# Two dense blocks on one core: second halves of weights later in the order, and a gated delta rule woven by another deal

## The chip, the cores and the metric

The kernel runs on one core of a Trainium2 chip. The metric is the device time of one execution in microseconds (us). Engines are named as in the profile: PE is TensorE's matmul, PEld its weight load, DVE is VectorE, ACT is ScalarE, POOL is GpSimd, SP is SyncE, whose queue issues the loads of the weights. Each engine takes its instructions in the order in which the program lists them.

## The reference, cut to what matters

Two blocks run one after the other on 256 tokens of width 1024. The first (attention and a mixture of 32 experts) is not touched. The second has two layers; the mixer of its first layer is a gated delta rule, of its second a block attention with rotary embedding ("moba"), and each is followed by a SwiGLU network.

```python
def gated_deltanet(x, w_in, w_conv, a_log, dt_bias, norm_g, w_out):
    proj = x @ w_in
    qkv, z, b_logit, a_in = jnp.split(proj, [...], axis=-1)
    qkv = jax.nn.silu(causal_depthwise_conv(qkv, w_conv))   # 4 taps, each channel by itself
    q, k, v = jnp.split(qkv, [GDN_QK, 2 * GDN_QK], axis=-1)
    q = l2_normalize(split_heads(q, nh)) * GDN_DK ** -0.5   # 8 heads of 128
    k = l2_normalize(split_heads(k, nh))
    v = split_heads(v, nh).astype(F32)
    beta = jax.nn.sigmoid(...)
    g = -(jnp.exp(a_log) * jax.nn.softplus(a_in + dt_bias))
    o = chunk_gated_delta_rule(q, k, v, g, beta)            # per head: triangular solve, recurrence
    o = o * lax.rsqrt(jnp.mean(o * o, -1, keepdims=True) + NORM_EPS) * norm_g
    o = o * jax.nn.silu(z)
    return o.reshape(bsz, seq, GDN_V) @ w_out

def second_block(x, ...):
    h = x
    for i in range(2):
        mix = gated_deltanet(h, ...) if i == 0 else moba_attention(h, ...)
        h = layer_norm(DEEPNORM_ALPHA * h + mix, ln1_g[i], ln1_b[i])
        h = layer_norm(DEEPNORM_ALPHA * h + swiglu(h, f_w13[i], f_w2[i]), ln2_g[i], ln2_b[i])
    return h
```

## The kernel before, in words

**Weights.** Every float32 product is made of three rounded products: a weight is split into a first half `wh` (ACT copies it to fp32r, line 1221: below "the cast") and a second half `wl` (the weight less `wh`, line 1224 on DVE, or on POOL while `hv.pool` is set: below "the second part"). `Stream` (lines 1204 to 1241) does this unit by unit: a unit is a quarter of a weight tile of up to 2 MB, and a ring of two places in SBUF holds the tiles. `_emit` lists the cast and the second part of one unit; after the last unit of a tile it calls `ring.free`, which issues the next load on SP's queue. `get` first fills a queue of units up to `ahead` + 1 and hands out the oldest.

**The delta rule** (`gdn`, from line 1444). The eight heads go in four pairs. `project(p)` makes q, k and v of a pair's two heads (48 steps of 768 columns on PE) and puts a generator `conv4` (line 1579) of each head on the list `late`: three first taps on ACT (line 1586), nine further taps on DVE (line 1584), then one SiLU on ACT (line 1595). `gates` also stands on `late`. `tick()` advances every generator on `late` by one step. `chunks(p)` (line 1609), below "the chain", is the delta rule of one pair: 26 steps, in each of which PE works on what DVE or ACT made in the step before. Its first two steps transpose (line 1620) and square (line 1623, ACT) the two heads, its third transposes the values (line 1629); the two buffers of the PSUM tile `tp` are used in turn, so the third step waits until ACT has finished the first head's squares and copy. POOL then takes the inverse root (line 328), lines 1657 and 1660 make the triangular matrices, lines 1677 to 1703 solve five levels (`X` and `W` in the trace: lines 1693 and 1703 on DVE), and lines 1718 to 1754 give the output.

**`weave`** (lines 1760 to 1788) sets the order by rounds. In a round each live chain advances by one step, and then a generator of other work ("the fill") is run for its share. The chains start in rounds 4, 12, 27 and 35. The fills are the projections of pairs 1, 2 and 3 (to be done by rounds 8, 23 and 31), the two other groups of z (round 45) and the first part of the output projection (round 65). The share is a fill's whole work over its rounds. After more than TICK = 1000 columns of fill comes a `tick`. Where a chain starts, `late` is emptied first. All of this stands in a manual schedule: on every engine the order of the program is the order of the queue.

**Boundaries** (`boundary`, lines 1300 to 1325) run the layer norm by an order written out by hand, also a manual schedule on PE, DVE and ACT: `... l01 b11 c00 h00 s10 f10 f11 x10 l10 x11 l11 h10`. The step `c00` takes four units from the stream for the next stage's first tile, `h00` multiplies them with the first 128 tokens, `s10`, `f10`, `f11` finish the norm of the other 128 tokens on DVE, `x10` and `x11` transpose them (line 413), `l10` and `l11` make their second halves (line 417), `h10` multiplies them. Outside manual schedules a planner orders the instructions.

Of the kernel before, what the change touches and what calls it, by code (L numbers as in the profile page):

```python
# [16 lines left out]
OP = mybir.AluOpType  # L17
# [20 lines left out]
TICK = 1000  # L38
# [4 lines left out]
LATE = 4  # L43
END = 7
SPLITS = 8
AHEAD = 4
FILL = 8


ORDER = "p00 p01 a00 b00 a01 b01 s00 p10 q11 f00 x00 r11 a10 f01 x01 l00 b10 a11 l01 b11 c00 h00 s10 f10 f11 x10 l10 x11 l11 h10"  # L50
# [150 lines left out]
def kernel(ctx: ExitStack, tc: tile.TileContext, a, out):  # L201
# [33 lines left out]
    for e in range(NE + 1):  # L235
        if e < NE:
            for k in range(4):
# [3 lines left out]
                src = w[:, k % 2 * TILE:(k % 2 + 1) * TILE].rearrange("p (k c) -> p k c", k=2)  # L241
# [29 lines left out]
    ring = Ring(nc, plan, both, n_block1, n_moe)  # L271
# [58 lines left out]
    def f32(ap):  # L330
        return ap.bitcast(F32)


    class Halves:


        def __init__(self, n_tiles, unit, first=0):

            self.first = first
            self.left, self.unit, self.ahead = n_tiles, unit, depth  # L340
            self.q, self.cur, self.pos = [], None, 0

        def _emit(self):
            if self.cur is None:
                if not self.left:
                    return False
                self.left -= 1
                self.cur, self.pos = ring.get(), 0
            src = self.cur[:, self.pos:self.pos + self.unit]
            shp = list(src.shape)  # L350
            n = int(np.prod(shp[1:]))
            wh = split.tile([128, 1024], F32R, name="wh")
            wl = split.tile([128, 1024], F32R, name="wl")
            if len(shp) == 4:
                s2 = src.rearrange("p a b c -> p (a b c)")
            else:
                s2 = src.rearrange("p a b -> p (a b)")
            nc.scalar.activation(wh[:, :n], s2, AF.Copy)  # L358
            eng = nc.gpsimd if self.first > 0 else nc.vector
            self.first -= 1  # L360
            eng.tensor_tensor(wl[:, :n], s2, f32(wh[:, :n]), op=OP.subtract)  # L361
            v = lambda t: t[:, :n].rearrange("p (u c) -> p u c", u=self.unit)
            self.q.append((v(wh), v(wl)))
            self.pos += self.unit
            if self.pos >= self.cur.shape[1]:
                self.cur = None
                ring.free()
            return True

        def get(self):  # L370
            while len(self.q) <= self.ahead and self._emit():
                pass
            return self.q.pop(0)
# [320 lines left out]
    def begun(g):  # L694

        next(g)
        go = lambda: next(g, None)
        return {H1: go, H2: go}


    rest = begun(qk_b(psB, 0, qB, 8))
# [5 lines left out]
    rest = begun(qk_b(ps, 1, kB, 2))  # L707
    rest = {0: restq, H1: rest[H1], H2: rest[H2]}
# [3 lines left out]
    for hp in range(4):  # L712
# [3 lines left out]
        for g in range(3):  # L716
            ps = mm_tiles()
            dense_tok(ps, hT_h, hT_l, hv, 8, 384, 2, hooks=rest)
            rest = {}
            if g < 2:  # L720
                rest = begun(qk_a(ps, g, (QA, KA)[g][hp]))
# [482 lines left out]
    class Stream:  # L1204


        def __init__(self):
            self.q, self.cur, self.pos, self.ahead = [], None, 0, AHEAD
            self.n, self.pool = 0, 0

        def _emit(self):
            if self.cur is None:
                if ring.at not in ring.tiles:
                    return False
                self.pos, self.cur = 0, ring.get()
                self.unit = {256: 4, 1024: 1}.get(self.cur.shape[2], 2)
            src = self.cur[:, self.pos:self.pos + self.unit].rearrange("p a b -> p (a b)")
            n = src.shape[1]
            w = splitp.tile([128, 2, 1024], F32R, name="wh")
            wh, wl = w[:, 0, :n], w[:, 1, :n]  # L1220
            nc.scalar.activation(wh, src, AF.Copy)  # L1221
            self.n = self.n + 1
            eng = nc.gpsimd if self.n % 3 < self.pool else nc.vector
            eng.tensor_tensor(wl, src, f32(wh), op=OP.subtract)  # L1224
            self.pos += self.unit
            if self.pos >= self.cur.shape[1]:
                ring.free()
                self.cur = None
            v = lambda t: t.rearrange("p (u c) -> p u c", u=self.unit)
            self.q.append((v(wh), v(wl)))  # L1230
            return True

        def fill(self, n):

            while len(self.q) < n and self._emit():
                pass

        def get(self):
            self.fill(self.ahead + 1)
            return self.q.pop(0)  # L1240

    hv = Stream()
# [45 lines left out]
    def mm3(o, xh, xl, wh, wl, k, t, nk):  # L1288

        ts_ = slice(t * 128, (t + 1) * 128)  # L1290
        nc.tensor.matmul(o, xh[:, k, ts_], wh, start=k == 0, stop=False)  # L1291
        nc.tensor.matmul(o, xh[:, k, ts_], wl, start=False, stop=False)  # L1292
        nc.tensor.matmul(o, xl[:, k, ts_], wh, start=False, stop=k == nk - 1)  # L1293
# [50 lines left out]
    class OutProj:  # L1344
# [29 lines left out]
        def second(self, ln, pool, head, row=None):  # L1374
            hv.fill(FILL - 4)
            boundary(Residual(ln, pool, row=row), lambda t, n: self.part(t, n, 0 if t else 2, 4), self.ps, head)
# [22 lines left out]
    def ffn(i, ln, last, head):  # L1399
        with tc.tile_pool(name="ff1_%d" % i, bufs=1, reuse_waits="tile") as fr, tc.tile_pool(name="ff2_%d" % i, bufs=2, reuse_waits="tile") as fw:  # L1400
# [24 lines left out]
            for k in range(22 - TAIL):  # L1425
                hv.ahead = min(FILL - 1, max(AHEAD, FILL - (22 - TAIL - k)))
                wh, wl = hv.get()
                for t in range(2):
                    for n in range(2):
                        c = slice(n * 512, (n + 1) * 512)  # L1430
                        mm3(pss[n][t], aT_h, aT_l, wh[:, 0, c], wl[:, 0, c], k, t, 22)
            hv.fill(FILL)
            hv.ahead = 0
# [10 lines left out]
    def gdn(head):  # L1444
        with tc.tile_pool(name="gd1", bufs=1, reuse_waits="tile") as gr, tc.tile_pool(name="gd2", bufs=2, reuse_waits="tile") as gw:
# [28 lines left out]
            zs, qkvs, op, oT, gated = [], {}, [], [], []  # L1474

            late = []

            def tick():
                late[:] = [g for g in late if next(g, 0) is None]
# [280 lines left out]
            def weave(chains, fills):  # L1760


                r, live, todo, base, done = 0, [], 0.0, 0, 0
                while chains or live or fills:
                    while chains and chains[0][0] <= r:
                        while late:
                            tick()
                        live.append(chunks(chains.pop(0)[1]))
                    if live:

                        hv.pool = 0

                    live = [g for g in live if next(g, 0) is None]
                    todo += fills[0][1] / (fills[0][0] - base) if fills else 0
                    while fills and todo > 0:
                        n = next(fills[0][2], None)
                        if n is None:
                            base = fills.pop(0)[0]
                            todo = 0 if base > r else todo
                            break  # L1780
                        todo -= n
                        done = done + n
                        if done > TICK:
                            done = 0
                            tick()
                    r += 1
# [266 lines left out]
```

## Time and profile before

| | us |
|---|---|
| median of 3 runs | 1931.11 |
| lowest, highest | 1929.81, 1931.31 |
| the profiled execution's own time | 1930.78 |
| its span, first to last instruction | 1929.1 |
| first block, to about | 1222 of the span |
| delta rule with its rounds, about | 1222 to 1422 |
| boundary, network, boundary | 1422 to 1630 |
| moba and boundary | 1630 to 1741 |
| network and end | 1741 to 1929 |

The rows further down come from the profile's page and from answers of the trace. A row of a timeline begins with its start and its duration; in brackets stands how long the engine was idle before it and which instruction released it. PEclk is the granted TensorE clock as a share of full speed.

### The profile page before, as it was taken

The numbers are of one execution on the slowest core, as the hardware profiler recorded it, in microseconds if no ns is written. First come the engines' busy times: TensorE is split into PE (matmuls) and PEld (weight loads), VectorE is DVE, ScalarE is ACT, GpSimd is POOL, SyncE is SP. The second block draws the span as 40 slices with busy tenths as digits, with TensorE's granted clock in tenths as the row PEclk, the third lists the DMA queues.
The fourth block names the chain that finished last, engine by engine and source line by source line (L and its number), as shares of the span: only waits on it lengthen the run. The fifth ranks groups of instructions, "written<-read, shape, count | busy, mean of one in ns | idle before, by whom it ended". The sixth has DMA issues, their size and how long they took to land.

```text
span 1929.1 us, 26325 instructions
## 1 busy us (share of the span) xinstructions
PE 1856.5 (96%) x11094; PEld 1243.2 (64%) x11094; DVE 856.2 (44%) x1633; ACT 597.6 (31%) x1060; POOL 98.7 (5%) x133
## 2 busy tenths in 40 slices
PE   9999999999999998999899998989899999999998
PEld 8888775444444443443333343879779988889996
DVE  7766563221232222122122132676665546666554
ACT  5544542111111111111111110645444443544441
POOL 3111000000000000000000000410010000000000
PEclk9999999999989999999999999999999999999999
DMA  7423489999999999999999999422425544535551
GB/s 276 161 112 132 185 350 383 428 430 431 430 432 429 432 430 430 431 429 432 430 431 429 433 429 395 176 100 102 154 71 214 185 186 177 197 131 202 190 197 45
DMA packets 36942, 561.35 MB, mean 291 GB/s; under 512 B 6321, under 2 KB 7361, under 8 KB 10194
## 3 DMA queue, kind: packets, MB, share of 16 engines
q1 hardware_dynamic: 35408, 553.17, 69.9%
q0 software_dynamic: 1264, 6.37, 0.9%
q8 instruction: 88, 1.44, 0.3%
q14 instruction: 36, 0.29, 0.0%
q10 hardware_dynamic: 146, 0.07, 0.0%
HBM read 558.55 MB, written 1.05 MB: 290 GB/s over the span
## 4 chain that ended last, share of the span: by engine, by line
PE 39%; DMA 13%; DVE 4%; ACT 2%; issue 1%; POOL 0%; POOLq 0%; SPq 0%; ACTq 0%; DVEq 0%
DMA ring<-in_w_gate_up_dram 10%; PE mm L986 7%; PE mm L1251 4%; PE mm L1252 4%; PE mm L1253 4%; PE mm L1291 4%; PE mm L1293 4%; PE mm L1292 4%; DMA ring<-in_w_down_dram 2%; DMA ring<-in_w_second_dram 1%; PE tp L972 1%; DVE wh L1224 1%; DVE big L1584 1%; PE mm L1124 1%; ACT wh L1221 1%
## 5 line engine op out<-in xcount | busy, mean ns | idle before, releaser
L986 PE MATMUL mm<-ring,hT_l 128*64 128x512 f32 x2048 | 483.2, 608 | 17.9 <-DMA ring<-in_w_gate_up_dram 11.0
L1224 DVE TENSOR_TENSOR wh<-ring,wh 128x1024 fp32r<-128x1024 f32 (+3 forms) x204 | 236.9, 1176 | 177.2 <-ACT wh L1221 177.0
L986 PEld LDWEIGHTS mm<-ring,hT_l 128*64 128x64 f32 x2048 | 154.9, 137 | 244.9 <-issue 221.1
L1221 ACT ACTIVATE wh<-ring 128x1024 fp32r<-128x1024 f32 (+3 forms) x216 | 215.8, 1014 | 188.9 <-PE mm L1293 74.2
L1124 PE MATMUL mm<-ring,oA_l 128*64 128x512 f32 x960 | 223.2, 602 | 18.3 <-DMA ring<-in_w_down_dram 18.2
L1251 PE MATMUL mm<-hT_h,wh 128*128 128x256 f32 x832 | 238.0, 286 | 1.2 <-DVE ik L1640 1.2
L1252 PE MATMUL mm<-hT_h,wh 128*128 128x256 f32 x832 | 235.3, 283 | 0.0
L1253 PE MATMUL mm<-hT_l,wh 128*128 128x256 f32 x832 | 235.2, 283 | 0.0
L1124 PEld LDWEIGHTS mm<-ring,oA_l 128*64 128x64 f32 x960 | 78.8, 138 | 150.8 <-issue 122.7
L1251 PEld LDWEIGHTS mm<-hT_h,wh 128*128 128x128 f32 x832 | 159.3, 192 | 2.5 <-issue 1.6
L1252 PEld LDWEIGHTS mm<-hT_h,wh 128*128 128x128 f32 x832 | 159.5, 192 | 0.0
L1253 PEld LDWEIGHTS mm<-hT_l,wh 128*128 128x128 f32 x832 | 159.4, 192 | 0.0
L1107 DVE SCALAR_TENSOR_TENSOR oA_h<-mm,gc,oA_h 128x512 fp32r<-128x512 f32 x32 | 24.0, 750 | 291.5 <-ACT oA_h L1106 291.5
L998 DVE TENSOR_TENSOR oB<-tp,hT_l 128x256 f32<-128x256 f32 x64 | 27.0, 422 | 225.9 <-PE tp L995 224.7
L393 PE MATMUL mm<-wl,hT_h 128*128 128x384 f32 (+2 forms) x304 | 108.7, 358 | 0.5 <-DVE wl L361 0.5
L392 PE MATMUL mm<-wh,hT_h 128*128 128x384 f32 (+2 forms) x304 | 106.5, 358 | 1.9 <-ACT wh L358 1.8
L394 PE MATMUL mm<-wh,hT_l 128*128 128x384 f32 (+2 forms) x304 | 107.1, 356 | 0.0
L361 DVE TENSOR_TENSOR wl<-ring,wh 128x768 fp32r<-128x768 f32 (+1 forms) x84 | 90.3, 1081 | 33.4 <-ACT wh L358 33.1
L358 ACT ACTIVATE wh<-ring 128x768 fp32r<-128x768 f32 (+1 forms) x86 | 79.9, 939 | 68.8 <-PE mm L394 63.4
L972 PEld LDWEIGHTS tp<-hT_l,hT_h 128*128 128x128 f32 x512 | 61.9, 191 | 50.5 <-issue 50.3
L1106 ACT ACTIVATE oA_h<-mm,gc 128x512 fp32r<-128x512 f32 x32 | 22.0, 687 | 224.4 <-PE mm L1124 224.4
L973 ACT ACTIVATE hT_l<-tp 128x256 f32<-128x256 f32 x64 | 24.6, 384 | 191.6 <-PE tp L972 191.6
(406 smaller groups left out, 2617.1 us busy)
## 6 DMA issues: line engine op xcount, KB each, us to landing
ring<-in_w_gate_up_dram SPq DMA_DIRECT2D x45, 4096.0 KB, 34.9
ring<-in_w_second_dram SPq DMA_DIRECT2D x42, 2048.0 KB, 7.8
ring<-in_w_down_dram SPq DMA_DIRECT2D x20, 4096.0 KB, 36.3
ring<-in_w_gate_up_dram SPq DMA_DIRECT2D x37, 2048.0 KB, 23.6
ring<-in_w_down_dram SPq DMA_DIRECT2D x22, 2048.0 KB, 39.2
ring<-in_w_first_dram SPq DMA_DIRECT2D x12, 1536.0 KB, 6.5
ring<-in_w_first_dram SPq DMA_DIRECT2D x8, 2048.0 KB, 7.8
ring<-in_w_second_dram SPq DMA_DIRECT2D x8, 1536.0 KB, 6.7
```

Of the source, the lines that this page charges most:

```text
L361: eng.tensor_tensor(wl[:, :n], s2, f32(wh[:, :n]), op=OP.subtract)
L392: nc.tensor.matmul(o, hs, wh[:, u], start=k == 0, stop=False)
L393: nc.tensor.matmul(o, hs, wl[:, u], start=False, stop=False)
L394: nc.tensor.matmul(o, ls, wh[:, u], start=False, stop=k == nk - 1)
L972: nc.tensor.matmul(tp[:, kk], h2[:, t, c], r, start=t == 0, stop=t == 1)
L986: nc.tensor.matmul(ps[n][64 * h:64 * h + 64], xk, w[:, n * 512:(n + 1) * 512], start=k == 0, stop=k == 7, skip_group_check=True)
L1124: nc.tensor.matmul(ps[n][64 * h:64 * h + 64], acts[e + h][:, k], w(h, k), start=k == 0, stop=k == 7, skip_group_check=True)
L1221: nc.scalar.activation(wh, src, AF.Copy)
L1224: eng.tensor_tensor(wl, src, f32(wh), op=OP.subtract)
L1251: nc.tensor.matmul(o, wh[:, u, c], xT_h[:, k + u], start=first, stop=False, skip_group_check=True)
L1252: nc.tensor.matmul(o, wl[:, u, c], xT_h[:, k + u], start=False, stop=False, skip_group_check=True)
L1253: nc.tensor.matmul(o, wh[:, u, c], xT_l[:, k + u], start=False, stop=k + u == 7, skip_group_check=True)
```

## The change

There are three edits. (1) In `Stream` the second part of a unit, and with it the `ring.free` of a tile's last unit, is put on the list when the next unit's cast is (`_end` in `_emit`), or when the unit is the only one left in the queue (`get`). (2) In `weave` the columns of a round are dealt by the number of chains that are at work in it: weights 2.0, 1.6, 1.0 and 0.7 for none, one, two and three; what is left of a fill is spread over its remaining rounds. (3) Except before the first chain, `tick()` can come after fewer columns than TICK, so that 11 ticks fit before the next chain starts.

```diff
--- before.py
+++ after.py
@@ -45,6 +45,9 @@
 SPLITS = 8
 AHEAD = 4
 FILL = 8
+
+STEPS = 26
+CONV = 11
 
 
 ORDER = "p00 p01 a00 b00 a01 b01 s00 p10 q11 f00 x00 r11 a10 f01 x01 l00 b10 a11 l01 b11 c00 h00 s10 f10 f11 x10 l10 x11 l11 h10"
@@ -1206,7 +1209,7 @@
 
         def __init__(self):
             self.q, self.cur, self.pos, self.ahead = [], None, 0, AHEAD
-            self.n, self.pool = 0, 0
+            self.n, self.pool, self.begun = 0, 0, None
 
         def _emit(self):
             if self.cur is None:
@@ -1221,15 +1224,27 @@
             nc.scalar.activation(wh, src, AF.Copy)
             self.n = self.n + 1
             eng = nc.gpsimd if self.n % 3 < self.pool else nc.vector
-            eng.tensor_tensor(wl, src, f32(wh), op=OP.subtract)
+            self._end()
             self.pos += self.unit
+            at = None
             if self.pos >= self.cur.shape[1]:
-                ring.free()
-                self.cur = None
+                at, self.cur = ring.at - 1, None
+
+            def end():
+                eng.tensor_tensor(wl, src, f32(wh), op=OP.subtract)
+                if at is not None:
+                    ring.free(at)
+            self.begun = end
             v = lambda t: t.rearrange("p (u c) -> p u c", u=self.unit)
             self.q.append((v(wh), v(wl)))
             return True
 
+        def _end(self):
+
+            if self.begun:
+                self.begun()
+            self.begun = None
+
         def fill(self, n):
 
             while len(self.q) < n and self._emit():
@@ -1237,6 +1252,8 @@
 
         def get(self):
             self.fill(self.ahead + 1)
+            if len(self.q) == 1:
+                self._end()
             return self.q.pop(0)
 
     hv = Stream()
@@ -1760,7 +1777,10 @@
             def weave(chains, fills):
 
 
-                r, live, todo, base, done = 0, [], 0.0, 0, 0
+                r, live, todo, done, used = 0, [], 0.0, 0, 0
+                starts = [c[0] for c in chains]
+
+                share = lambda r: (2.0, 1.6, 1.0, 0.7)[sum(s <= r < s + STEPS for s in starts)]
                 while chains or live or fills:
                     while chains and chains[0][0] <= r:
                         while late:
@@ -1771,16 +1791,24 @@
                         hv.pool = 0
 
                     live = [g for g in live if next(g, 0) is None]
-                    todo += fills[0][1] / (fills[0][0] - base) if fills else 0
+                    if fills:
+                        left = fills[0][1] - used
+                        rest = sum(share(x) for x in range(r, max(fills[0][0], r + 1)))
+                        todo = todo + left * share(r) / rest if left > 0 else 1.0
+
+                    every = TICK
+                    if late and chains and chains[0][0] > LATE:
+                        every = min(TICK, max(todo, 256.0) * (chains[0][0] - r) / CONV)
                     while fills and todo > 0:
                         n = next(fills[0][2], None)
                         if n is None:
-                            base = fills.pop(0)[0]
-                            todo = 0 if base > r else todo
+                            fills.pop(0)
+                            todo, used = min(todo, 0.0), 0
                             break
                         todo -= n
+                        used += n
                         done = done + n
-                        if done > TICK:
+                        if done > every:
                             done = 0
                             tick()
                     r += 1
```

## Rows read from the trace of the kernel before

**Rows 1.** The page, busy time of the engines; share of the span, instructions:
```profile
PE 1856.5 (96%) x11094; PEld 1243.2 (64%) x11094; DVE 856.2 (44%) x1633; ACT 597.6 (31%) x1060; POOL 98.7 (5%) x133
```

**Rows 2.** Busy time by stretch; columns us, engines, PEclk, DMA share, GB/s:
```profile
1250.00:1284.00 34.00, 27.24 (x264) 25.68 (x262) 24.93 (x58) 22.49 (x66) 7.09 (x9) 1.00 0.33 123
1284.00:1340.00 56.00, 54.34 (x768) 50.89 (x769) 38.92 (x85) 23.16 (x65) 6.42 (x11) 1.00 0.23 82
1340.00:1389.00 49.00, 43.66 (x573) 39.02 (x572) 37.86 (x80) 23.57 (x63) 4.73 (x8) 0.97 0.40 148
1389.00:1422.00 33.00, 30.36 (x286) 24.93 (x284) 11.52 (x21) 14.28 (x44) 2.44 (x4) 0.95 0.22 73
...
1470.00:1490.00 20.00, 20.00 (x170) 20.00 (x168) 10.47 (x10) 9.33 (x12) 0.00 (x0) 1.00 0.57 211
```

**Rows 3.** Waits of PE, 1222 to 1422; columns total us, times, longest us:
```profile
PE sc L1677 <- ACT wh L1221: 3.5, 1, 3.5
...
PE sc L1700 <- DVE X L1693: 3.3, 2, 2.6
...
PE sc L1677 <- DVE W L1703: 2.0, 3, 1.4
...
PE sc L1677 <- DVE X L1706: 2.0, 3, 1.6
```

**Rows 4.** Waits of DVE, the same stretch:
```profile
DVE wh L1224 <- ACT wh L1221: 25.6, 15, 5.9
```

**Rows 5.** Timeline of ACT; columns start us, us, instruction, idle and its releaser:
```profile
1247.14 0.82 ACT L1586 ACTIVATE big<-mm,conv 128x256 f32<-128x256 f32 x2
...
1256.70 0.83 ACT L1595 ACTIVATE big<-big 128x768 f32<-128x768 f32 x1
...
1257.43 0.26 ACT L1623 ACTIVATE gsq<-tp 128x128 f32<-128x128 f32 x1
...
1258.70 0.87 ACT L1221 ACTIVATE wh<-ring 128x768 fp32r<-128x768 f32 x1
```

**Rows 6.** Timeline of PE, rounds 5, 6 and 14:
```profile
1257.58 0.66 PE L1620 MATMUL tp<-ident,big 128*128 128x128 f32 x4 [1.72 <-ACT big L1595]
...
1260.22 0.60 PE L1629 MATMUL tp<-ident,big 128*128 128x128 f32 x4
...
1284.20 0.39 PE L1677 MATMUL sc<-W,LT 64*64 64x64 f32 x6 [1.44 <-DVE W L1703]
```

**Rows 7.** Timeline of DVE (a first tap, four taps) and POOL (the power):
```profile
1248.00 0.48 DVE L1584 SCALAR_TENSOR_TENSOR big<-mm,conv,big 128x255 f32<-128x255 f32 x1 [4.86 <-ACT big L1586]
...
1277.69 1.90 DVE L1584 SCALAR_TENSOR_TENSOR big<-mm,conv,big 128x253 f32<-128x253 f32 x4
...
1261.70 1.67 POOL L328 TENSOR_TENSOR rr<-rr,mhalf 128x8 f32<-128x8 f32 x1
```

**Rows 8.** Timeline of DVE, round 37:
```profile
1360.44 4.63 DVE L1224 TENSOR_TENSOR wh<-ring,wh 128x1024 fp32r<-128x1024 f32 x4 [1.86 <-ACT wh L1221]
```

**Rows 9.** Busy time in stretches of 5 us with the granted clock:
```profile
1360.00:1365.00 5.00, 2.27 (x39) 1.92 (x38) 4.56 (x5) 3.57 (x5) 0.34 (x2) 1.00 0.70 298
1365.00:1370.00 5.00, 4.19 (x55) 3.68 (x56) 3.13 (x7) 0.73 (x1) 0.00 (x0) 0.71 0.81 275
...
1405.00:1410.00 5.00, 3.49 (x21) 3.17 (x22) 1.84 (x4) 0.66 (x3) 0.00 (x0) 0.81 0.00 0
1410.00:1415.00 5.00, 5.00 (x32) 4.53 (x31) 1.23 (x1) 2.58 (x7) 0.00 (x0) 0.85 0.02 5
```

**Rows 10.** Timeline of DVE and PE at two boundaries:
```profile
1437.49 0.75 DVE L1284 SCALAR_TENSOR_TENSOR acc<-acc,lnrs,dT 128x512 f32<-128x512 f32 x1
...
1439.18 1.29 DVE L417 TENSOR_TENSOR hT_l<-tp,hT_h 128x512 fp32r<-128x512 f32 x2 [0.22 <-ACT hT_h L415]
...
1623.73 1.21 DVE L1224 TENSOR_TENSOR wh<-ring,wh 128x1024 fp32r<-128x1024 f32 x1
...
1628.94 0.63 PE L413 MATMUL tp<-ident,acc 128*128 128x128 f32 x4 [0.82 <-DVE acc L1284]
```

## The prediction

> **What bounds the kernel now.** I read the page's busy times first: PE is busy for 96% of the span [rows 1], so what can be won or lost is mostly PE's waiting. Next the busy times by stretch: in the networks PE never rests and takes 170 matmuls of 256 columns in 20 us, 0.118 us each [rows 2]; there a cast or a second part is made units ahead, and their order can't matter. In the delta rule, PE lacks 6.8 us in the rounds up to 13, 1.7 in rounds 14 to 30, 5.3 in rounds 31 to 46 and 2.6 to the end [rows 2]. Then the waits of PE: each is one step of a chain that waits for DVE or ACT [rows 3]. Last the waits of DVE: in 15 places it stood for 25.6 us before a second part whose cast was not made, with the chain's own DVE work behind it in the queue [rows 4]. So the stage goes at the pace of PE where the fill between two steps covers the way over DVE, and at the pace of DVE's and ACT's queues where it doesn't.
>
> **The change part by part.** I stepped both versions of the loop by hand, round by round, for the order on each engine.
>
> *The first chain (rounds 0 to 13).* No chain is at work in rounds 0 to 3, so they get 36,864 x 2.0/14.4 = 5120 columns each, not 4608: 27 steps of the projection by the end of round 3, not 24. The first head of pair 1 is then already projected, its convolution is on `late`, and the emptying of `late` at round 4 lists all of it, nine taps and a SiLU, ahead of the chain's first squares. Before, `late` was empty there and the squares followed the SiLU of head 1 directly [rows 5]. Now ACT does, after that SiLU: a cast (0.73, to 1258.2), three first taps of 0.4 (two took 0.82 [rows 5]; to 1259.4), and then waits for DVE's nine taps. A tap on DVE began at 1248.00, released by ACT, just as the second of two first taps ended [rows 5, 7]; so the nine begin at 1259.0, take 0.475 each by four in 1.90 [rows 7] and end at 1263.3. SiLU 0.75, to 1264.0; squares and copy 1.27 as before [rows 5], to 1265.3. PE reaches the third step (line 1629) at 1260.2 as before [rows 6]: its wait of 1.72 for the SiLU is shorter, but two more units of fill stand ahead. It then stands for 5.1 us, since `tp` has two buffers.
>
> Why the first of these two PSUM reads doesn't release DVE is not in the rows. The Trainium skill, PSUM — Partial Sum Buffer, PSUM bank collisions raise a hardware error, has a rule that speaks against the change here: two engines must not touch one bank at a time, reads included, so tools order them. q and k of a head lie in one bank. With the rule the stand is 5.1 us; if DVE could read beside ACT it would be 4.7.
>
> Against the stand: with taps done early and two second parts fewer ahead of `X`, the later waits of this stretch (2.6, and 1.4 before 1284.20 [rows 3, 6]) shrink. Stepped on: second squares to 1267.4, POOL's root to 1269.4 (1.67 [rows 7]), the triangular matrix to 1272.7, seven more taps and three second parts on DVE, `X` at 1281.1, line 1700 at 1281.5 after a wait of 1.7, and round 14 at 1284.2 with 69 steps of fill done, where it was 1284.2 with 70. A step is three matmuls, 0.36 [rows 2]: net +0.4.
>
> A stand of that length has a price. After PE was busy for only 2.27 of 5 us, the granted clock of the next 5 us was 0.71, a stretch at the lower of its two levels, 1.2 GHz instead of 2.4 [rows 9]; after the waits of 2.6 and 1.4 it stayed 1.00 [rows 2]. The pair around 1410 lost (1 - 0.81 + 1 - 0.85) x 5 = 1.7 us [rows 9]. 5.1 us is longer than the stand that was followed by it (3.5 [rows 3]); I take +1.7, with 0 as the other end, since rows show no stand of this length at this place. The Trainium skill, TensorE: Matmul & The Clock Gate, What's actually happening, has the slow level as the default and activity as what lifts it. By that rule the end at 0 falls away; the sum stays.
>
> *Rounds 14 to 31.* The same 26 and 48 steps of fill with the same chain steps. Nine matmuls of fill (1.25 us) per round throughout leave round 18 short: DVE has a second part and one tap more ahead of `X`, PE waits 0.55. Rounds 24 to 30 get 15 to 24 matmuls instead of 18, which takes away the 0.3 before round 31. The wait of about 1.1 there stays, as no fill is left for round 31 in either version. Net +0.1; bounds -1 and +1.
>
> *Rounds 32 to the end.* Before, PE's stands here are 3.5 in round 39, behind four second parts of 4.63 us in one row on DVE [rows 3, 8], 1.6 in round 54 (the longest of the last row of [rows 3]), 0.7 in round 36 (3.3 less 2.6 [rows 3]), about 0.4 and 0.6 more, and twice 1.7 for the clock: 10.2. After: in round 36 two taps and the SiLU are still in front at the emptying of round 35, 1.9; the four second parts are now parted, three ahead of `W` in round 41 (3 x 1.15 [rows 8], less the fill: 1.5) and one ahead of `X` in round 42 (1.3); rounds 49 and 52 get no fill, 0.6 and, with the gating of pair 2 ahead of `W`, 1.4: together 6.7. No stand is over 2 us, but the last rounds stay thin, so I take half of one slow stretch, 0.85. Net 7.55 - 10.2 = -2.65; bounds -5.8 (no stand of mine comes, none of the clock) and 0. The loads keep their lead: the last load for the output projection is issued one unit later, in round 39, and the cast that needs it holds up nothing that PE wants within its time.
>
> *The three boundaries with a next stage.* The stream is filled ahead of them; the second part of the last unit filled now waits for `get`, that is for `c00`, which stands on DVE right in front of `s10`. One more second part goes there: 1.12 us by the one that already stands there at 1623.73 [rows 10]. Behind it are the norm of the second 128 tokens, the transposes, `l10` and `h10`. At the middle boundary PE already waits 0.82 for this chain [rows 10], so the whole 1.1 is on the path. At the other two DVE ends the norm at 1438.2 and goes on with line 417 at 1439.2 [rows 10], some 0.3 to 0.9 of slack, of which the first product uses up most: 0.8 each. Sum +2.7; bounds 0 and 3.4. The place that it left, ahead of the boundary, was not on the path: there PE's products end last.
>
> *The rest.* In networks and moba the planner can list second parts by their new place; PE is full in the networks. I take 0, bounds -1 and +1.
>
> **Sum:** 0.4 + 1.7 + 0.1 - 2.65 + 2.7 + 0 = +2.25, from the profiled execution's 1930.78 to 1933.0. The median of the runs shown is 0.33 above that execution, so 1933.4; I call it 1933.
>
> **The rivals.** *Faster:* the delayed second part is what matters. Wherever DVE stood in front of one [rows 4], the chain's work now goes first, and the stands of 3.5 and 1.6 with both slow stretches (3.4) go without new ones: -8.5; with +2.7 at the boundaries -5.8, 1925.3. For it: the 25.6 us. Against: by the order three second parts still stand in one row in round 39, and DVE's whole work is the same.
>
> *Slower:* the convolution in front of the first chain is not paid back. If the stretch to round 14 is held by the late squares (root, triangular matrix, all of the solve) and not by DVE's backlog, the 5.1 us less the two steps done (0.7) and 1.7 of clock stay: +6.1, and with -2.65 and +2.7 it is +6.15, 1936.9. It decides at round 14: the first line-1677 step that was at 1284.20 [rows 6] would come after 1287. For it: DVE is idle while ACT catches up. Against: DVE was busy for 24.9 of these 34 us [rows 2], and with the taps done early it has less left.
>
> That the convolutions are not spread is part of the forecast: for the first chain the deal does the reverse.
>
> **How the numbers follow.** Forecast (within 0.2%, 3.9 us, about what a measurement can tell): 0.44. Faster rival 0.28, slower rival 0.28. The likeliest one's own range is 1929.5 to 1935. Over all I give 1924.5 to 1938.0: it takes in both rivals and about a tenth is left beyond each end.
>
> **What would show it.** Right: a stand of PE of 4 to 5.5 us at the first step of line 1629 after nine taps in one row on DVE; a slow stretch behind it; no stand over 2 us in rounds 36 to 42; a second line-1224 instruction between line 1272 and 1277 at the middle boundary, and one at each of the other two, with `h10` about 1 us later. Wrong: PE passing round 6 without a stand, the boundaries as long as before, or a stage that ends more than 5 us off.

## The result and the profile after

| | us |
|---|---|
| before, median of 6 runs | 1931.19 (1929.81 to 1931.68) |
| after, median of 6 runs | 1941.43 (1939.25 to 1942.21) |
| ratio after to before, 95% interval | 1.0054 [1.0043, 1.0064] |
| profiled execution after: own time, span | 1941.94, 1940.3 |

The change makes the kernel 10 us slower; the forecast of 1933.0 and its range up to 1938.0 missed that. PE's busy share is where it was [rows 1], so the loss must be looked for stage by stage:

```profile
PE 1862.0 (96%) x11094; PEld 1246.9 (64%) x11094; DVE 854.5 (44%) x1632; ACT 597.5 (31%) x1060; POOL 101.4 (5%) x134
```

Seven places on PE can be found in every kernel of this study: the first product after the first block's last transposes (1221.91 us before, 1221.53 after), the last transposes of the delta rule (1420.47, 1422.86), the first product of `h10` at each boundary (1439.20, 1445.05; 1629.32, 1637.41; 1738.89, 1749.94), and the first transposes of the second and third boundary (1618.75, 1624.34; 1728.98, 1738.37). The stretches between them, after less before:

| stretch | forecast, us | measured, us |
|---|---|---|
| delta rule | 0.4 + 1.7 + 0.1 - 2.65 = -0.45 | +2.78 |
| first boundary | +0.8 | +3.45 |
| first network | 0 | -0.25 |
| second boundary | +1.1 | +2.50 |
| moba, behind it | 0 | +1.30 |
| third boundary | +0.8 | +1.66 |
| start and last network | 0 | -0.28 |
| sum | +2.25 | +11.16 |

**The delta rule.** The same stretches as in [rows 2], after (the columns are those of [rows 2]):

```profile
1250.00:1284.00 34.00, 26.40 (x216) 25.22 (x214) 21.16 (x52) 18.18 (x45) 8.68 (x9) 0.90 0.33 124
1284.00:1340.00 56.00, 54.67 (x780) 51.19 (x781) 38.19 (x82) 26.57 (x84) 6.77 (x12) 0.97 0.22 79
1340.00:1389.00 49.00, 43.84 (x572) 39.92 (x571) 35.70 (x81) 22.55 (x61) 5.11 (x8) 0.97 0.41 151
1389.00:1422.00 33.00, 31.17 (x324) 25.64 (x321) 13.78 (x25) 15.93 (x46) 2.44 (x4) 1.00 0.01 2
```

PEclk is what differs most: 0.90 in the first row, where it was 1.00. PE's timeline in rounds 5, 6 and 14 (to set beside [rows 6]; L1637, L1646 and L1694 were 1620, 1629 and 1677):

```profile
1257.50 0.66 PE L1637 MATMUL tp<-ident,big 128*128 128x128 f32 x4 [0.56 <-ACT big L1612]
...
1265.60 1.12 PE L1646 MATMUL tp<-ident,big 128*128 128x128 f32 x4 [5.30 <-ACT kf L1641]
...
1288.82 0.68 PE L1694 MATMUL sc<-W,LT 64*64 64x64 f32 x16
```

DVE and ACT just ahead of that stand: the nine taps; the first taps, the SiLU and the end of the squares:

```profile
1258.93 4.37 DVE L1601 SCALAR_TENSOR_TENSOR big<-mm,conv,big 128x255 f32<-128x255 f32 x9 [4.96 <-ACT big L1603]
```

```profile
1258.08 1.18 ACT L1603 ACTIVATE big<-mm,conv 128x256 f32<-128x256 f32 x3
...
1263.39 0.84 ACT L1612 ACTIVATE big<-big 128x768 f32<-128x768 f32 x1 [4.13 <-DVE big L1601]
...
1265.14 0.40 ACT L1641 ACTIVATE kf<-tp 128x256 f32<-128x256 f32 x1
```

The stand is there, step for step: taps at 1258.93 (forecast 1259.0), SiLU at 1263.39 (1263.3), 5.30 us of idle PE (5.1). What follows it, in stretches of 5 us:

```profile
1260.00:1265.00 5.00, 0.30 (x3) 0.09 (x1) 3.16 (x7) 1.60 (x8) 0.11 (x1) 0.96 0.33 140
1265.00:1270.00 5.00, 4.40 (x21) 4.41 (x22) 2.43 (x4) 4.77 (x17) 2.31 (x5) 0.50 0.00 0
1270.00:1275.00 5.00, 5.00 (x39) 5.00 (x39) 1.90 (x6) 1.93 (x4) 0.27 (x1) 0.86 0.00 2
1285.00:1290.00 5.00, 5.00 (x60) 4.68 (x55) 2.08 (x4) 4.12 (x21) 1.32 (x2) 0.66 0.00 0
```

From 1260 to 1275 the granted clock is short by (0.04 + 0.50 + 0.14) x 5 = 3.4 us. The stretch at the lower level begins 1.0 us before the stand ends, where PE had no work to lose, so 2.9 us are lost on PE's work. At 1285 it is again 0.34 x 5 = 1.7, though PE is busy without a gap in that row; it had waited 1.91 us for `X` until 1284.57. Round 14's step comes at 1288.82, past the 1287 that the slower rival named.

**The first boundary.** The chain that ended last, in order of time (start, us, what; PE's products left out). It is ACT and DVE, where before PE's products ended last:

```profile
1431.89 0.52 ACT wh L1224
1432.41 0.43 issue
1432.84 1.98 ACT wh L1224 x2
1434.83 0.49 ACT hT_h L418
...
1437.22 1.14 DVE wh L1234
1438.36 0.60 DVE hT_l L420
1438.96 0.60 DVE bnst L1289
1439.56 1.12 DVE wh L1234
...
1444.66 0.63 PE tp L416 x4
```

Two second parts (L1234) stand in the norm's chain, not one, and ahead of them three casts stand in front of the copy of the transposed norm (L418). The order of DVE's instructions in the program, with the units' names, says which second parts these are. That at 1439.56 is the one that `c00` lists, as forecast. That at 1437.22 belongs to the last of the four units that the boundary itself fills at its end. In the code that fill stands in a block, `with tc.issue_after(last_of(DVE))`, which keeps it behind the boundary; the change lists its last second part at the next call, outside the block, and the planner put it forward. The casts are late for a third reason, seen in the DMA share of the stretches 1388 to 1396 and 1412 to 1432; first before, then after:

```profile
1388.00:1396.00 8.00, 8.00 (x97) 6.91 (x98) 3.28 (x7) 2.86 (x7) 0.00 (x0) 1.00 0.72 264
```

```profile
1388.00:1396.00 8.00, 7.38 (x108) 6.14 (x108) 5.70 (x10) 3.49 (x7) 0.00 (x0) 1.00 0.01 3
...
1412.00:1423.00 11.00, 10.89 (x60) 8.99 (x59) 3.38 (x6) 5.75 (x20) 1.21 (x2) 1.00 0.01 2
1423.00:1432.00 9.00, 8.17 (x37) 6.07 (x38) 6.51 (x10) 0.81 (x2) 1.30 (x2) 1.00 0.64 233
```

The load of the network's second tile waits for the second part of the output projection's last unit. That unit stays the last one cast until the queue is empty, so its second part now comes at 1422 and the load runs until about 1431.8, the moment at which the three casts start.

**The other two.** DVE at the second boundary, and PE with the clock behind it:

```profile
1629.32 2.34 DVE L1234 TENSOR_TENSOR wh<-ring,wh 128x1024 fp32r<-128x1024 f32 x2
...
1634.65 1.22 DVE L1234 TENSOR_TENSOR wh<-ring,wh 128x1024 fp32r<-128x1024 f32 x1
1635.78 0.74 DVE L1301 SCALAR_TENSOR_TENSOR acc<-acc,lnrs,lnrow 128x512 f32<-128x512 f32 x1
```

```profile
1636.67 1.09 PE L416 MATMUL tp<-ident,acc 128*128 128x128 f32 x4 [1.83 <-DVE acc L1301]
```

```profile
1635.00:1640.00 5.00, 3.33 (x10) 2.87 (x11) 3.70 (x5) 1.56 (x3) 0.00 (x0) 0.66 0.99 423
```

The forecast had the two in one row; the third, between the norm's last two instructions, is the one that left its block. PE's stands of 0.80 and 1.83 us are followed by a stretch that costs 0.34 x 5 = 1.7 us, 0.4 of it still in the boundary and 1.3 in moba. The same two stands (0.85 and 1.83) in run e1 below are followed by none:

```profile
1628.92 0.63 PE L416 MATMUL tp<-ident,acc 128*128 128x128 f32 x4 [1.83 <-DVE acc L1301]
```

```profile
1628.00:1633.00 5.00, 4.08 (x20) 3.49 (x21) 4.16 (x6) 0.81 (x2) 0.00 (x0) 1.00 0.98 418
```

At the third boundary of the change there are two second parts again, and a table load of ACT, new in this place (before, it ran at 1732.67, while ACT had nothing else to do):

```profile
1742.05 1.22 DVE L1234 TENSOR_TENSOR wh<-ring,wh 128x1024 fp32r<-128x1024 f32 x1
...
1744.38 1.21 DVE L1234 TENSOR_TENSOR wh<-ring,wh 128x1024 fp32r<-128x1024 f32 x1
```

```profile
1749.39 1.28 ACT L1424 ACT_TABLE_LOAD   x1
```

### The profile page after: what moved, and what is told of

It is laid out like the page before. It is cut to its first block, busy times and chain, and to the rows that moved or that the text cites. A ratio compares the mean times of both kernels' runs of the same rounds, so it can differ in the third digit from the quotient of the medians.

```text
span 1940.3 us, 26330 instructions
## 1 busy us (share of the span) xinstructions
PE 1862.0 (96%) x11094; PEld 1246.9 (64%) x11094; DVE 854.5 (44%) x1632; ACT 597.5 (31%) x1060; POOL 101.4 (5%) x134
## 4 chain that ended last, share of the span: by engine, by line
PE 40%; DMA 13%; DVE 4%; ACT 1%; issue 1%; POOL 1%; POOLq 0%; SPq 0%; ACTq 0%; DVEq 0%
DMA ring<-in_w_gate_up_dram 10%; PE mm L989 7%; PE mm L1268 5%; PE mm L1269 5%; PE mm L1270 5%; PE mm L1308 4%; PE mm L1310 4%; PE mm L1309 4%; DMA ring<-in_w_down_dram 2%; DMA ring<-in_w_second_dram 1%; PE tp L975 1%; PE mm L1127 1%; DVE wh L1234 1%; PE sc L1694 1%; DVE big L1601 1%
## 5 line engine op out<-in xcount | busy, mean ns | idle before, releaser
L1234 DVE TENSOR_TENSOR wh<-ring,wh 128x1024 fp32r<-128x1024 f32 (+3 forms) x203 | 236.1, 1176 | 159.2 <-ACT wh L1224 159.2
```

## The experiments

Theory A: two things carry the loss, the convolution that is emptied ahead of the first chain (with the clock behind it), and pending second parts that land in the boundaries. Rival B: the new deal carries all of it. The first four runs part them; the others part the pieces. In the table every stretch is given against before; "clock" is what the stretches at the lower clock cost within the delta rule of that profiled execution, half of the time in which PE worked in them (3.4 before, 6.3 with the change), and "less clock" what is left of its difference without them. The change and e8 have the same order in the delta rule and still differ by 0.6 in that column, so smaller differences there say nothing.

| run | median, us | ratio, 95% interval | delta rule | clock | less clock | boundaries 1, 2, 3 | moba |
|---|---|---|---|---|---|---|---|
| the change | 1941.4 | 1.0054 [1.0043, 1.0064] | +2.8 | 6.3 | -0.1 | 3.45, 2.50, 1.66 | +1.3 |
| e1 | 1934.6 | 1.0025 [1.0016, 1.0034] | -4.1 | 3.4 | -4.1 | 3.39, 2.14, 1.67 | +0.1 |
| e2 | 1933.1 | 1.0013 [1.0004, 1.0022] | +3.2 | 6.4 | +0.2 | 0, 0, 0 | 0 |
| e3 | 1932.5 | 1.0010 [1.0001, 1.0019] | +2.8 | 6.2 | -0.1 | 0, 0, 0 | 0 |
| e4 | 1936.2 | 1.0028 [1.0017, 1.0039] | -5.4 | 1.7 | -3.7 | 5.56, 2.49, 1.67 | +1.25 |
| e5 | 1926.3 | 0.9979 [0.9970, 0.9988] | -3.8 | 3.4 | -3.8 | 0, 0, 0 | 0 |
| e6 | 1927.3 | 0.9980 [0.9971, 0.9989] | -1.8 | 5.1 | -3.5 | 0, 0, 0 | 0 |
| e7 | 1928.1 | 0.9988 [0.9979, 0.9997] | -2.7 | 3.4 | -2.7 | 0, 0, 0 | 0 |
| e8 | 1936.1 | 1.0027 [1.0015, 1.0039] | -0.75 | 2.1 | +0.5 | 2.20, 1.14, 0.57 | 0 |
| e9 | 1936.6 | 1.0024 [1.0013, 1.0034] | +2.8 | 6.3 | -0.1 | 0, 1.11, 1.11 | +1.6 |
| e10 | 1937.6 | 1.0034 [1.0022, 1.0047] | +2.4 | 6.0 | -0.2 | 1.70, 2.14, 1.67 | +0.1 |
| e11 | 1925.6 | 0.9974 [0.9964, 0.9983] | -4.7 | 3.2 | -4.5 | 0, 0, 0 | 0 |
| e12 | 1930.3 | 1.0003 [0.9994, 1.0012] | +0.3 | 5.1 | -1.4 | 0, 0, 0 | 0 |

**e1: the first edit alone** (`Stream` of after, `weave` of before).

> The change's first edit alone (second parts one unit later), with the weave of before. Theory A (the change loses at the three boundaries, because second parts that are listed later land in the norm's chain on DVE and the last load comes late): the boundaries cost what they cost with the whole change, 3.6 + 2.5 + 1.65 us, and about 1.3 for the clock behind the second one; the weave, whose emptying at round 4 is that of before, is within 2 us of before. 1931.2 + 9 = about 1940, between 1937 and 1942. Rival B (the new deal of columns carries the loss, and the boundaries are late only because the weave ended in another state): within 1.5 us of before.

Measured 1934.6: below the range of theory A, and not rival B. The boundaries cost what they cost with the whole change, but for the slow clock behind the second, which did not come in this execution; what I had wrong is the delta rule, which gains 4.1 us. DVE's wait in front of second parts falls from 25.6 us [rows 4] to:

```profile
DVE wh L1234 <- ACT wh L1224: 9.5, 4, 5.9
```

But the gain does not lie where the faster rival put it. Round 14's step comes 60.1 us after the first product, where it was 62.3: 2.2 of the 4.1 us are won before it. The stand of 3.5 us in round 39 [rows 3] is still there with 2.7; the trace now puts it down to `W`, which stands on DVE behind three second parts in one row; that of 1.6 in round 54 is unchanged, and so are the two slow stretches. PE's wait, and DVE's row ahead of it:

```profile
PE sc L1694 <- DVE W L1720: 3.1, 2, 2.7
```

```profile
1356.35 3.50 DVE L1234 TENSOR_TENSOR wh<-ring,wh 128x1024 fp32r<-128x1024 f32 x3 [1.42 <-ACT wh L1224]
```

So the faster rival had about half of its 8.5 us in the weave of before, by luck: at other places than those it named. The boundaries hid it.

**e2: the other two edits alone** (`Stream` of before, `weave` of after).

> The second and third edits alone (new deal of columns, more ticks), with every second part right behind its cast. Theory A: the three boundaries as before, no second part within the norm's chain; the weave costs what it cost with the whole change, +2.4 us at the last transposes, with a stand of about 5 us at the first chain's third step and the lower clock behind it: 1931.2 + 2.4 = about 1933.6, between 1932 and 1936. Rival B: about 1940.

1933.1, as theory A has it. The stand is the same one, 5.3 us, and so is the clock behind it. The losses of e1 and e2 sum to 7, not 10: behind the stand the later second parts win only 0.4 us (delta rule +3.2 and +2.8), not 4.1. The slow clock at the second boundary works the other way: it costs the change 1.7 us and e1 nothing.

**e3: the change, with pending second parts listed in time.**

```diff
 hv.fill(FILL - 4)
+hv._end()
...
 hv.fill(FILL)
+hv._end()
...
     with tc.issue_after(last_of(mybir.EngineType.DVE)):
         hv.fill(AHEAD)
+        hv._end()
...
 wh, wl = hv.get()
+hv._end()
```

The first two stand ahead of the boundaries (`OutProj.second`, `ffn`), the third at a boundary's end, the last in `OutProj.first`.

> The whole change, but the pending second part is listed at three places: at the end of each stretch in which units are filled ahead of a boundary, within the block that holds the fill at a boundary's end behind DVE's last instruction, and right after each unit taken by the output projection's first part. Theory A: all 7.75 us of the three boundaries and the 1.3 of the slow clock behind the second go, the weave stays: 1941.4 - 9 = about 1932.4, between 1931 and 1934.5. Rival B (boundaries late because of how the weave ends): above 1938.

1932.5: all three boundaries and moba go back to their length before, to 0.03 us.

**e4: the change, emptying only what the starting chain needs.**

```diff
-while late:
-    tick()
-live.append(chunks(chains.pop(0)[1]))
+p = chains.pop(0)[1]
+while any(owner.get(id(g), 0) <= p for g in late):
+    tick(p)
+live.append(chunks(p))
```

`owner` holds the pair of each convolution, and `tick(p)` advances only what belongs to pairs up to p.

> The whole change, but where a chain starts only the convolutions that it needs are emptied; one of a later pair that has begun goes on by ticks. Theory A (the stand at the first chain's third step comes from the nine taps and the SiLU of a head that the chain doesn't need): the stand of 5.3 us falls under 2, the two stretches at the lower clock (6.8 and 3.4 us) go, the second step of the first level comes at about 1284.5 instead of 1288.8, and the time falls by 4 to 6.5 us, to about 1936. Rival C (the later part of this stretch is held by DVE's backlog anyway, so the taps come back as a wait before round 14): the stand goes, but the step at round 14 stays after 1287 and the time falls by less than 2.

1936.2, as theory A has it. PE's third step of the first chain, and the stretches to set beside those of after:

```profile
1260.36 0.60 PE L1649 MATMUL tp<-ident,big 128*128 128x128 f32 x4
```

```profile
1260.00:1265.00 5.00, 5.00 (x45) 5.00 (x44) 4.39 (x10) 4.30 (x15) 2.74 (x6) 1.00 0.41 175
1265.00:1270.00 5.00, 4.69 (x40) 4.51 (x40) 4.81 (x13) 3.40 (x6) 0.16 (x1) 1.00 0.02 5
```

No stand, and no loss of clock in these two rows; 1.7 us are lost from 1279 on, behind a wait of 2.94 for `X`. The delta rule gets 8.2 us shorter than with the whole change, more than I expected; 2.1 of it are given back in the first boundary, where now a slow stretch falls (0.50 from 1430 to 1435). Rival C falls: without the stand the step of round 14 comes at 1282.22.

**e5 and e6: both repairs; and the first edit alone with e3's lines.**

> The whole change with the two repairs together: pending second parts listed ahead of the boundaries, within the block at a boundary's end and in the output projection; and only the convolutions that a starting chain needs are emptied. Theory A: the weave keeps what it had with the second repair alone (5.4 us shorter than before the change), the boundaries are as before, the clock falls at no boundary: 1930.4 - 5.4 = about 1925.0, between 1923.5 and 1927. Rival D (the stretch of 6.8 us at the lower clock seen in the first boundary belongs to the thin rounds at the end of the weave, not to the boundary's waits): it comes again and costs 3.4, so 1927.5 to 1929.

> The first edit alone (second parts one unit later) with the pending ones listed at the boundaries as in the run with the repairs; weave of before. Theory A: the weave keeps its 4.1 us of gain and the 7.2 us of the boundaries go: 1930.4 - 4.1 = about 1926.3, between 1925 and 1928. Rival F (the gain in the weave was a loan: second parts not yet listed at its end have only been pushed into the boundary, and come back when they are listed in time): above 1929.

Both beat the kernel before and the changed one, e5 at 1926.3 and e6 at 1927.3, in their ranges. The slow stretch of e4's boundary is not in e5's profiled execution, and 1926.3 lies below rival D's 1927.5, so rival D falls as far as one trace can show. Rival F falls too: the weave's gain stays when the boundaries are as before. Less clock, e6 has 3.5 and e5 3.8.

**e7: the deal with e4's repair, every second part right behind its cast.**

> The second and third edits with the emptying limited to the convolutions that a starting chain needs; every second part right behind its cast. Theory G (deal and later second parts win different waits, so their gains add): the deal by itself is then worth 5.4 - 4.1 = 1.3 us, about 1929.1. Theory E (both take away the same waits, of DVE's queue in front of X and W; behind the stand the later second parts were worth 0.4): the deal alone has nearly the whole gain, about 1925.5. In between, 1927 to 1928, neither is shown.

1928.1, between the two theories: -2.7 less clock. Later second parts add about 1.1 to it (e5), so the two edits win partly the same waits; neither theory is shown.

**e8, e9, e10: the three places of e3, one at a time.**

> The whole change with one repair only: the second part of the last unit that is filled at a boundary's end is listed within the block that keeps this fill behind DVE's last instruction. Theory A (this second part leaves the block, and is put into the norm's chain, at all three boundaries): each boundary gets about 1.1 us shorter and at the second PE's wait gets so short that no slow clock follows it: 3 x 1.1 + 1.3, or 4.6 us less than the change, 1.0054 x 1930.4 - 4.6 = about 1936.3, between 1935 and 1938.5. Rival H (only the second part taken with the four units of the next stage counts, the other lies beside PE's products): within 1.2 us of the change, above 1939.5.

> The whole change with one repair only: the pending second part is listed after the units filled ahead of a boundary, not with the four units that the next stage takes between the two halves of the norm. Theory A: the second L1234 instruction in front of the second half of the norm goes at all three boundaries, each gets about 1.1 us shorter (what is left of 3.45, 2.50 and 1.66 with the other repair alone was 2.20, 1.14 and 0.57), PE's wait at the second boundary gets short, and about 4 us of the change go: 1940.7 - 4 = 1936.7, between 1934.5 and 1938.5. Rival (one second part fits beside PE's products, only the second of two is on the path): under 1 us each, above 1938.5.

> The whole change with one repair only: in the output projection's first part the pending second part is listed right after each unit taken, and with it the load that follows the last unit. Theory A (the load issued late holds three casts on ACT in front of the copy of the transposed norm, and PE behind that): the three casts come before 1431, the first boundary goes from 3.45 to about 2.3 us over before, the other two stay at 2.5 and 1.7; the time falls by about 1.2, to 1939.5, between 1938 and 1941. Rival I (the load lies beside the second parts, which end last anyway): the first boundary stays over 3.1.

e8 (listed within the block) takes 1.25, 1.36 and 1.09 us off the three boundaries (0.4 of the 1.36 is slow clock, which did not come): the second parts that left their block were nearly half of the boundaries' cost. At the second boundary PE's wait of 1.83 falls to 0.82. That moba loses nothing here is not shown to come from that, since it loses nothing in e1 and e10 either. Its first boundary keeps the late casts, and the row names the load:

```profile
1428.06 2.96 ACT L1224 ACTIVATE wh<-ring 128x1024 fp32r<-128x1024 f32 x3 [7.52 <-DMA ring<-in_w_second_dram]
1430.92 0.57 ACT L418 ACTIVATE hT_h<-tp 128x512 fp32r<-128x512 f32 x1
```

e10 (listed in the output projection) has its load done by 1407; the casts go one by one as places come free, as they did before, and the first boundary loses 1.75 us of its 3.45 (1.2 were expected), so rival I falls. Its 1937.6 lies below the range of theory A; no slow stretch came at its second boundary:

```profile
1428.04 1.06 ACT L1224 ACTIVATE wh<-ring 128x1024 fp32r<-128x1024 f32 x1 [4.87 <-PE mm L1310]
1429.44 1.06 ACT L1224 ACTIVATE wh<-ring 128x1024 fp32r<-128x1024 f32 x1 [0.34 <-PE mm L1310]
1430.84 1.06 ACT L1224 ACTIVATE wh<-ring 128x1024 fp32r<-128x1024 f32 x1 [0.34 <-PE mm L1310]
1431.81 0.58 ACT L418 ACTIVATE hT_h<-tp 128x512 fp32r<-128x512 f32 x1
```

e9 (listed ahead of the boundary) gave more than its 1.1 us at the first boundary, namely all 3.45: with that second part out of the way the planner put the late casts, all four, behind the copies, and the stray second part behind the norm:

```profile
1434.54 0.60 ACT L418 ACTIVATE hT_h<-tp 128x512 fp32r<-128x512 f32 x1 [1.51 <-PE tp L416]
1435.27 3.90 ACT L1224 ACTIVATE wh<-ring 128x1024 fp32r<-128x1024 f32 x4
```

So the three causes don't add up at the first boundary; how much each takes there depends on where the planner puts the rest. Part of the gain is given back: the first network, 0.25 us shorter than before with the change, is 0.46 longer here. At the second boundary e9 takes 1.39 us (0.3 of it clock) and at the third only 0.55, where 1.1 each were expected; there its part and e8's add up to the whole, without the clock. The slow stretch behind the second boundary came here too, against theory A.

**e11 and e12: e5 without the third edit; e5 with equal weights.**

> The run with both repairs (1926.3), without the third edit: a tick after every 1000 columns throughout, so that at round 12 three taps and a SiLU of the second pair stand ahead of its squares. Theory A: as with the first chain, but short: DVE takes 1.4 and ACT 0.75 for them, of which other work on PE covers most; within 1.5 us of the run with both repairs, 1926 to 1928. Rival J (what stands ahead of a chain's squares decides, however short): over 2 us longer, above 1928.5.

> The run with both repairs (1926.3) with equal weights for all rounds in the second edit: no head of a later pair is projected before the first chain starts. Theory A (once the emptying is limited, the unequal deal wins little: before and after it differ by 0 to 2 us in the weave when stretches at the lower clock are left aside): 1926 to 1928.5. Rival K (the unequal deal is what shortens the weave): above 1929.5, near the time of the kernel before.

e11 is the fastest kernel of the study, 1925.6; the intervals of e5 and e11 overlap, so the spread convolutions win nothing that shows here, and rival J falls. e12 lands on rival K's side: 1930.3, no faster than before. Of the 4 us to e5, 1.7 are clock and 2.4 are not. But e6, whose deal is that of before, has 3.5 less clock where e12 has 1.4; what in e12 takes the other 2 us (the more frequent ticks, or the new way of carrying a round's rest) no run tells apart.

## Why the prediction was wrong, point by point

Of the 8.9 us between forecast and measurement 4.9 lie in the boundaries, 1.3 in moba behind the second one and 3.2 in the delta rule; the networks and the start take back 0.5.

**The three boundaries: the step that failed.** It was forecast that "one more second part goes there: 1.12 us", with a sum of 2.7 and an upper bound of 3.4; measured 7.6 (0.4 of it slow clock), and 1.3 of the same slow stretch in moba. The second part at `c00` was right in mechanism and place; where it is left alone, at e8's second and third boundary, it costs 1.14 and 0.57 us (1.1 and 0.8 forecast). Two more things of the same edit were not in the sum: the last second part of the boundary's own fill, which left the block that held it back (e8: 1.25, 1.0 without the clock, and 1.09 us), and the load behind the output projection's last unit, which runs some 35 us later (e10: 1.75 us). Both were in the code and in the diff: the forecast followed the pending second part to the first place where it is listed, and not to every place where the stream stops. On loads it said that they "keep their lead" and looked only at the last load for the output projection; the load after that lost it. The bound of 3.4 was worked out for one second part at each boundary, so it could not hold.

**The first chain.** The stand was forecast at 5.1 us and came at 5.3; DVE's taps began as the second of ACT's first taps ended, so it is the 5.1 and not the 4.7 of a DVE that reads beside ACT. Its price in clock was mis-sized: +1.7 with 0 as the other end, measured 2.9 behind it and 1.7 more from 1285.1 to 1288.5. The bounds went from rows of the kernel before, whose longest stand there was 3.5 us [rows 3, 9]; a stand longer than every row should have had its other end above the row, not only below. The rest of the term was +0.4, and that was about right: the lag at round 14 is 67.29 - 62.29 = 5.0 us from the first product, without the clock 5.0 - 2.9 - 1.7 = 0.4, plus one step of fill (0.36) not yet done: 0.8.

The Trainium skill, TensorE: Matmul & The Clock Gate, What's actually happening, has the slow level as the default. By that rule the end at 0 falls away, and the trace agrees: all six profiled executions with the stand (the change, e2, e3, e8 to e10) have a slow stretch at its end that costs 2.1 to 3.0 us of PE's work, and e4, e5 and e7, without it, show 1.00 from 1260 to 1270.

**The later rounds.** Rounds 14 to 31: +0.1 forecast, +0.25 measured. Rounds 32 to the end: -2.65 forecast, -2.5 measured, of which 1.7 are one slow stretch less than before. These two sums held. One sign did not: the stand in round 36, forecast at 1.9, came at 2.26 us, against "no stand over 2 us", with the slow stretch from 1360 behind it. And the lower bound of -5.8 does not follow from its own words: with no stand and no slow clock the term would be -10.2.

**The rivals.** The slower rival's sign came true at its own point (1288.82, after 1287), but not for its reason: of the 5.0 us of lag there 4.6 are clock and 0.4 late squares. e8 has the same order up to there and no slow stretch at 1285. It passes the point 65.3 us after its first product, 3.0 later than before, and 2.1 of that are clock. So the sign could not tell late squares (4.4 us by the rival, 0.4 to 0.8 measured) from clock:

```profile
1286.62 0.68 PE L1695 MATMUL sc<-W,LT 64*64 64x64 f32 x16
```

The faster rival was ruled down because "three second parts still stand in one row in round 39". e1 bears that out, three in one row with a stand of 2.7 us behind them, and shows that the later second parts win 4.1 us in the weave of before all the same, most of it elsewhere. Its gain was lost to the stand and to the boundaries that I had under-priced, and the range was too narrow above.

**What stays open.** Why slow stretches come at 1285 and 1360 in one execution and not in another of the same order: e3 loses 1.7 us at each, e8 at neither. PE's waits for `X` ahead of them are the same, 1.91 us until 1285.00 and 2.26 until 1359.52 in e3, 1.92 until 1283.88 and 2.27 until 1356.90 in e8. The stretch behind the second boundary is like this too: it comes in the change, e4 and e9 and not in e1 and e10. No run here shows what decides it.

```profile
1285.00:1290.00 5.00, 5.00 (x62) 4.68 (x63) 2.12 (x4) 4.06 (x21) 0.81 (x2) 0.66 0.00 0
1360.00:1365.00 5.00, 5.00 (x56) 4.47 (x53) 2.18 (x6) 4.01 (x16) 2.77 (x3) 0.66 0.01 3
```

```profile
1285.00:1290.00 5.00, 5.00 (x77) 4.60 (x75) 1.98 (x3) 4.96 (x19) 2.55 (x5) 1.00 0.02 3
1360.00:1365.00 5.00, 5.00 (x74) 4.39 (x71) 2.35 (x5) 3.26 (x9) 2.49 (x5) 1.00 0.00 0
```

The first pair is e3, the second e8. It may also be why the times of one kernel spread here, in e8 from 1932.9 to 1937.5; that is not shown, since one execution of each kernel has a trace.

## What to carry to other kernels

When an instruction is listed "one later", go through every place where the list stops (the end of a fill, of a block, of an order written by hand) and ask what is left pending there, what its release lets go (a load), and whether a block that held it still does. Empty ahead of a chain only what that chain reads. And take a stretch's difference apart into clock and the rest before comparing two profiles.

## What was not expected of the hardware

A stand of 5.3 us on PE was followed by a stretch at the lower clock that cost 2.1 to 3.0 us of PE's work, where one of 3.5 us had cost 1.7 before. And after the same waits of 1.9 and 2.3 us PE, busy for 5.00 us in 5 us, ran at a granted clock of 0.66 in one execution and at 1.00 in another.
